# A third of the first out-projection moved into the mLSTM, and the S5 phasor table mirrored by another engine

## The chip, the cores and the metric

The kernel runs on one core of one Trainium2 chip. The metric is device time in microseconds for one execution. The engines are TensorE (PE in the profile; its weight loads are PEld), VectorE (DVE), ScalarE (ACT), GpSimd (POOL) and SyncE (SP, which here only issues DMAs); all run their own queue of instructions in order and wait for each other by semaphores.

## The reference

One inference step of a two-layer encoder for two request groups: a prompt of 2048 tokens behind 16 meta tokens, and 8 decode streams of 16 tokens. Layer 0 runs an S5 state-space mixer (512 columns wide) and an mLSTM (1024 columns wide) side by side; layer 1, retention and RG-LRU, is untouched by the change. What matters here:

```python
def even_layer(h, g, i, st, P, segments):
    u = rmsnorm(h, g)
    ua, za, xb, zb = jnp.split(u @ P['ev_w_in'][i], [W_A, 2 * W_A, 2 * W_A + W_B], axis=-1)
    ya, s_re, s_im = s5_mixer(ua, ...)
    yb, mc, mn, mm, mbuf = mlstm_mixer(xb, ...)
    gated = jnp.concatenate([ya * jax.nn.silu(za), yb * jax.nn.silu(zb)], axis=-1)   # 512 + 1024 columns
    h = h + gated @ P['ev_w_out'][i]                                                 # (1536, 1024)
```

The mLSTM is a recurrence over chunks of tokens with a 256x256 state per head and four heads. The out-projection's 1536 rows are 12 blocks (k) of 128: k 0 to 3 are the S5 third, k 4 to 11 belong to the mLSTM.

## The kernel before

The kernel is written as a sequence of phases inside one `tile.TileContext(schedule_with_timeline_sim=True)`: a scheduler with a simulated timeline sets the order of the instructions on each engine, the pools' buffers set what must wait for what. In the profile the phases lie at: `phase_in0` 0 to about 247 us (first in-projection), the S5 scan and the mLSTM's projections to about 885, `phase_mlstm` about 893 to 1203, `phase_out0` to about 1620, then layer 1.

**Number format.** Products that need more than one pass are split: `split` casts an operand to fp32r on ScalarE (`h`) and subtracts on VectorE or GpSimd (`l`), and `mm3` (L123 to L125) does three matmuls: h x h, h x l, l x h.

**The phasor table.** In `phase_in0`, at its second block, `s5_turns` builds for the S5 scan a table of rotations in four rounds of 8 groups. In each, VectorE fills the upper half of `s5tb` by repeated complex products (L557 to L562), ScalarE writes the mirrored lower half in two instructions (L744), and a DMA of 1032 KB in ScalarE's queue stores it to `d_rot` (L745). The pool of `s5tb` is closed after that, and its memory goes, among others, to `wfh`/`wfl`, the first split weights of the next phase, which therefore wait for the last store. ScalarE also issues the many `d_ua` stores (L305) at the end of the phase; SyncE issues the loads of the next phase (`wr`, `wv`, `ut`, `bif`), and GpSimd subtracts its split weights (L118).

**The mLSTM.** `phase_mlstm` goes over 17 tiles of 128 tokens, one in unit 0 and two in each of units 1 to 8. `ml_scores` of the next unit is written ahead of `ml_heads` of the current one. `ml_scores` does 48 matmuls of 256 columns (L123 to L125 on `m_xch`/`m_xcl`), transposes (L1214) and the score product (L1231); `ml_heads` does, for each of four heads, the output product into `pn` (L1361, L1363), two updates `pc` of the state `ct` (L1366, read by VectorE at L1370), the normalisation on VectorE and GpSimd (L1247 to L1255) and, at the end of a tile, eight transposes of `m_yn` into `pa` (L1269), which VectorE reads at L1272. The PSUM buffers are three `pn`, two `pc` and three `pa`. The split weights `wo0` to `wo3` of the out-projection are loaded in units 2 to 5 and those of k 4 to 7 in the last one. Behind the units come k 0 to 7 of the first out-projection tile (`e.first`, on `m_xc`) and the final state (L1426, eight pairs of products through `pc`).

**The out-projection.** `phase_out0` goes over the 17 tiles (and the 16 meta tokens) in the order that `out_tiles` gives. For a tile `out_operands` loads the 12 blocks (k 0 to 3 from `d_ya`, the rest from `d_gb`, L1466) and splits them, and `out_mm` does 2 halves x 12 k x 3 matmuls of 512 columns. `put` adds the residual on VectorE (L1502) and stores the tile to `d_h`. In the same loop the decode streams' mLSTM step (`ml_running`) advances by one piece for each of the first tiles: it loads the states `m_c` (L1307), updates and stores them, and GpSimd copies their columns to `ncol` (L1330). From the 13th tile on parts of the next in-projection take its place.

## Time and profile before

| what | value |
|---|---|
| time, median of 3 runs (lowest, highest) | 3130.14 us (3120.72, 3131.16) |
| the profiled execution | 3125.61 us |
| its span | 3123.9 us |
| TensorE busy | 2995.7 us, 96% of the span |
| VectorE, ScalarE, GpSimd busy | 1717.8 us (55%), 1062.8 us (34%), 970.9 us (31%) |
| DMA traffic | 404.82 MB, mean 130 GB/s |

The profiled execution is one run of its own; its time is 1.7 us more than the span that the trace covers. A busy share is an average over stages with different limits, so the stretches of the trace are read one by one below. The granted clock of TensorE has two levels, 2.4 GHz (1.00 in the profile) and 1.2 GHz; a mean between them says for how much of a stretch each held.

### The profile page before, as it was taken

The numbers are of one execution on the slowest core, as the hardware profiler recorded it, in microseconds if no ns is written. First come the engines' busy times: TensorE is split into PE (matmuls) and PEld (weight loads), VectorE is DVE, ScalarE is ACT, GpSimd is POOL, SyncE is SP. The second block draws the span as 40 slices with busy tenths as digits, with TensorE's granted clock in tenths as the row PEclk, the third lists the DMA queues.
The fourth block names the chain that finished last, engine by engine and source line by source line (L and its number), as shares of the span: only waits on it lengthen the run. The fifth ranks groups of instructions, "written<-read, shape, count | busy, mean of one in ns | idle before, by whom it ended". The sixth has DMA issues, their size and how long they took to land.

```text
span 3123.9 us, 45398 instructions
## 1 busy us (share of the span) xinstructions
PE 2995.7 (96%) x17435; PEld 2709.9 (87%) x17435; DVE 1717.8 (55%) x3482; ACT 1062.8 (34%) x1868; POOL 970.9 (31%) x1152
## 2 busy tenths in 40 slices
PE   8996999998999899999999999999999999999999
PEld 8996998997988887767799999999998898888887
DVE  4275885554547885233356666766610026665664
ACT  4223343335244433211235555555521112211221
POOL 6104664546436654111102111111100014433432
PEclk9998999998989999999999999999999999999999
DMA  6437555557634545665541111111122158544442
GB/s 214 120 100 210 158 168 151 164 165 159 209 91 149 171 153 171 212 196 169 152 147 59 48 49 52 51 52 52 43 84 75 52 157 249 140 127 131 135 124 75
DMA packets 447299, 404.82 MB, mean 130 GB/s; under 512 B 43593, under 2 KB 392977, under 8 KB 447082
## 3 DMA queue, kind: packets, MB, share of 16 engines
q1 hardware_dynamic: 335340, 272.36, 30.6%
q10 hardware_dynamic: 111742, 129.56, 12.4%
q8 instruction: 137, 2.24, 0.3%
q14 instruction: 80, 0.66, 0.1%
HBM read 266.35 MB, written 135.49 MB: 129 GB/s over the span
## 4 chain that ended last, share of the span: by engine, by line
PE 60%; DVE 8%; DMA 3%; issue 1%; ACT 1%; POOL 0%; SPq 0%; DVEq 0%; ACTq 0%; POOLq 0%
PE p_pm L124 8%; PE p_pm L125 8%; PE p_pm L123 8%; PE r_pm L125 4%; PE r_pm L124 4%; PE r_pm L123 4%; PE pa L123 3%; PE pa L124 3%; PE pa L125 3%; DVE p_d L1714 1%; PE pn L1363 1%; PE pc L1366 1%; DMA m_rw<-d_grow 1%; PE r_o L1916 1%; DVE m_qs L1206 1%
## 5 line engine op out<-in xcount | busy, mean ns | idle before, releaser
L123 PE MATMUL p_pm<-pu,p_wh 128*128 128x384 f32 (+1 forms) x1568 | 512.1, 327 | 0.2 <-ACT pu L105 0.2
L124 PE MATMUL p_pm<-pu,p_wh 128*128 128x384 f32 (+1 forms) x1568 | 511.8, 327 | 0.0
L125 PE MATMUL p_pm<-pu,p_wl 128*128 128x384 f32 (+1 forms) x1568 | 511.3, 326 | 0.0
L123 PE MATMUL pm<-ub,wh 128*128 128x384 f32 (+1 forms) x1136 | 378.6, 334 | 1.6 <-ACT vo L453 1.6
L124 PE MATMUL pm<-ub,wh 128*128 128x384 f32 (+1 forms) x1136 | 377.6, 332 | 1.6 <-DVE ub L109 1.6
L125 PE MATMUL pm<-ub,wl 128*128 128x384 f32 (+1 forms) x1136 | 375.2, 332 | 0.0
L123 PEld LDWEIGHTS p_pm<-pu,p_wh 128*128 128x128 f32 x1568 | 294.2, 188 | 1.8 <-issue 1.2
L124 PEld LDWEIGHTS p_pm<-pu,p_wh 128*128 128x128 f32 x1568 | 294.5, 188 | 1.0 <-issue 0.8
L125 PEld LDWEIGHTS p_pm<-pu,p_wl 128*128 128x128 f32 x1568 | 294.4, 188 | 0.0
L118 POOL TENSOR_TENSOR wl<-wr,wh 128x256 fp32r<-128x256 f32 x188 | 174.7, 959 | 222.4 <-ACT wh L105 222.4
L123 PEld LDWEIGHTS pm<-ub,wh 128*128 128x128 f32 x1136 | 216.3, 191 | 6.6 <-issue 4.0
L124 PEld LDWEIGHTS pm<-ub,wh 128*128 128x128 f32 x1136 | 216.3, 190 | 3.0 <-DVE ub L109 2.1
L124 PE MATMUL r_pm<-rol,r_gh 128*128 128x512 f32 x544 | 217.7, 401 | 1.1 <-POOL rol L109 0.6
L123 PE MATMUL r_pm<-roh,r_gh 128*128 128x512 f32 x544 | 217.9, 401 | 0.8 <-ACT p_o L1624 0.8
L125 PE MATMUL r_pm<-roh,r_gl 128*128 128x512 f32 x544 | 217.0, 400 | 0.7 <-DVE r_gl L109 0.7
L125 PEld LDWEIGHTS pm<-ub,wl 128*128 128x128 f32 x1136 | 215.9, 190 | 1.7 <-issue 1.6
L109 POOL TENSOR_TENSOR p_wl<-p_wr,p_wh 128x1024 fp32r<-128x1024 f32 x34 | 82.1, 2417 | 384.1 <-ACT p_wh L105 373.1
L109 POOL TENSOR_TENSOR p_xcl<-p_xc,p_xch 128x384 fp32r<-128x384 f32 (+1 forms) x48 | 46.8, 974 | 244.7 <-ACT p_xch L105 208.1
L125 PEld LDWEIGHTS r_pm<-roh,r_gl 128*128 128x128 f32 x544 | 102.9, 189 | 22.6 <-DVE r_gl L109 1.2
L124 PEld LDWEIGHTS r_pm<-rol,r_gh 128*128 128x128 f32 x544 | 102.9, 189 | 21.6 <-POOL rol L109 1.0
L123 PEld LDWEIGHTS r_pm<-roh,r_gh 128*128 128x128 f32 x544 | 102.7, 189 | 21.7 <-ACT p_o L1624 1.2
L1714 DVE RECIPROCAL p_d<-p_d 128x384 f32<-128x384 f32 (+1 forms) x48 | 116.7, 2430 | 0.6
(732 smaller groups left out, 6821.6 us busy)
## 6 DMA issues: line engine op xcount, KB each, us to landing
wr<-in_ev_w_in_dram SPq DMA_DIRECT2D x47, 512.0 KB
p_wr<-in_od_w_in_dram SPq DMA_DIRECT2D x40, 512.0 KB
d_in<-p_o ACTq DMA_DIRECT2D x80, 192.0 KB
m_rw<-d_grow SPq DMA_DIRECT2D x18, 512.0 KB
s5u<-d_ua SPq DMA_DIRECT2D x32, 274.0 KB
d_v<-vo ACTq DMA_DIRECT2D x68, 128.0 KB
m_va<-d_v SPq DMA_DIRECT2D x17, 512.0 KB
d_h<-o_x ACTq DMA_DIRECT2D x17, 512.0 KB
```

Of the source, the lines that this page charges most:

```text
L109: (nc.gpsimd if pool else nc.vector).tensor_tensor(l, x, h, op=OP.subtract)
L118: nc.gpsimd.tensor_tensor(out[:, c], a[:, c], b[:, c], op=op)
L123: nc.tensor.matmul(out, a[0], b[0], start=start, stop=False, **kw)
L124: nc.tensor.matmul(out, a[0], b[1], start=False, stop=False, **kw)
L125: nc.tensor.matmul(out, a[1], b[0], start=False, stop=stop, **kw)
L1206: v.tensor_tensor(qs[:, 4 * j:4 * j + 4, :n].rearrange("p (h m) n -> p h m n", m=2), qt[j][:, :, cs].rearrange("p (h m) n -> p h m n", m=2 ...
L1363: nc.tensor.matmul(pn[:n], c.qs[:, 2 * h + k, :n], ct[h][:, k, :], start=False, stop=k == 1)
L1366: nc.tensor.matmul(pc, c.kw[:n, h, 128 * k:128 * (k + 1)], c.va[:n, h, :], start=True, stop=True)
L1714: v.reciprocal(d[:, :n], d[:, :n])
L1916: nc.tensor.matmul(po, qk[:, h, :], S[:, h, :], start=False, stop=True)
```

## The change

The S5 third of the out-projection is computed tile by tile inside the mLSTM. `first_part`, called once for each of the 17 tiles after its unit's heads, loads the tile of `d_ya` (256 KB), splits it on ScalarE and VectorE, does 2 halves x 4 k x 3 matmuls of 512 columns into a new PSUM buffer `pf`, copies each half with ScalarE, and stores it (ScalarE's queue) to a new DRAM tensor `d_hp`. The room in PSUM comes from `pc`, which has one buffer instead of two. The weights `wo0` to `wo3` are loaded ahead of the units. In the out-projection only k 4 to 11 remain; each tile loads its rows of `d_hp` (512 KB, L1514 of the new kernel) and GpSimd adds them to the residual (L1515). In `s5_turns` the mirror is done by GpSimd, and the store is issued by SyncE.

```diff
@@ s5_turns
             for i in range(2):
-                nc.scalar.mul(tb[:, i, :, 0:MID][:, :, ::-1], tb[:, i, :, MID + 1:], 1.0 - 2 * i)
-            nc.scalar.dma_start(e.rot[:, :, gs, :], tb)
+                nc.gpsimd.tensor_scalar(tb[:, i, :, 0:MID], tb[:, i, :, MID + 1:][:, :, ::-1], 1.0 - 2 * i, None,
+                                        op0=OP.mult)
+            nc.sync.dma_start(e.rot[:, :, gs, :], tb)
@@ -1385,10 +1386,31 @@
         wo.append((h, l))
 
     with P(e, "m_sb", 2) as sb, PS(e, "m_ps") as ps:
-        pn, pa = psum(ps, pn=3, pc=2), psum(e.pa, pa=3)
+        pn, pa = psum(ps, pn=3, pc=1, pf=1), psum(e.pa, pa=3)
         pt = lambda nm, *shape: (pa if nm == "pa" else pn)(nm, *shape)
         units = [[1]] + [[s, s + 1] for s in range(2, 18, 2)]
         nxt = ml_scores(e, sb, lp, ow0, pt, units[0])
+        for k in range(4):
+            r = sb.tile([128, D], F32, name="m_zb", bufs=2)
+            nc.sync.dma_start(r, out_w(e)[:, k, :])
+            weights(k, r, *(ow0.tile([128, D], F32R, name=f"wo{x}{k}") for x in "hl"))
+
+        def first_part(c0, n, kind, row):
+
+            g = sb.tile([128, 4, 128], F32, name="m_fg")
+            h, l = (sb.tile([128, 4, 128], F32R, name="m_f" + x) for x in "hl")
+            nc.sync.dma_start(g, e.ya[:, :, c0:c0 + n])
+            split(nc, h, l, g)
+            for q in range(2):
+                qs = slice(512 * q, 512 * q + 512)
+                pf = pn("pf", 512)
+                for k in range(4):
+                    mm3(nc, pf, (h[:, k], l[:, k]), (wo[k][0][:, qs], wo[k][1][:, qs]), k == 0, k == 3)
+                o = sb.tile([128, 512], F32, name="m_fo")
+                nc.scalar.copy(o, pf)
+                nc.scalar.dma_start(e.hp[c0:c0 + n, qs], o)
+
+        rest = out_tiles(e)
         for i in range(len(units)):
             cur = nxt
             if i + 1 < len(units):
@@ -1404,16 +1426,12 @@
                         weights(k + j, r[:, j, :], *(ow0.tile([128, D], F32R, name=nm, bufs=b) for _ in range(2)))
             for c in cur:
                 ml_heads(e, c)
-            if 2 <= i < 6:
-
-                r = sb.tile([128, D], F32, name="m_zb", bufs=2)
-                nc.sync.dma_start(r, out_w(e)[:, i - 2, :])
-                weights(i - 2, r, *(ow0.tile([128, D], F32R, name=f"wo{x}{i - 2}") for x in "hl"))
+                first_part(*rest.pop(0))
         t = out_tiles(e)[0]
         e.first = out_operands(e, lambda j, nm: lp.tile([128, 12, 128], F32 if nm == "g" else F32R, name="m_xc",
                                                         bufs=3), 1, *t)
         e.pms = [pa("pa", 512) for _ in range(2)]
-        for k in range(8):
+        for k in range(4, 8):
             for q in range(2):
                 out_mm(e, e.pms[q], t[1], e.first, k, q)
 
@@ -1457,21 +1475,21 @@
 
 def out_operands(e, room, parts, c0, n, kind, row):
 
-    m = 12 // parts
+    m = 8 // parts
     r = []
     for j in range(parts):
         g, h, l = (room(j, nm) for nm in "ghl")
         for k in range(0, m, 4):
             f = m * j + k
-            e.nc.sync.dma_start(g[:, k:k + 4, :n], e.gb[:, f - 4:f, c0:c0 + n] if f else e.ya[:, :, c0:c0 + n])
-        split(e.nc, h[:, :, :n], l[:, :, :n], g[:, :, :n])
+            e.nc.sync.dma_start(g[:, k:k + 4, :n], e.gb[:, f:f + 4, c0:c0 + n])
+        split(e.nc, h[:, :m, :n], l[:, :m, :n], g[:, :m, :n])
         r += [(h[:, k, :n], l[:, k, :n]) for k in range(m)]
     return r
 
 
 def out_mm(e, pm, n, g, k, q):
     qs = slice(512 * q, 512 * q + 512)
-    mm3(e.nc, pm[:n], g[k], (e.wo[k][0][:, qs], e.wo[k][1][:, qs]), k == 0, k == 11)
+    mm3(e.nc, pm[:n], g[k - 4], (e.wo[k][0][:, qs], e.wo[k][1][:, qs]), k == 4, k == 11)
 
 
 DSTEPS = 1
@@ -1491,7 +1509,10 @@
 
         def residual(c0, n, kind, row):
             h1 = sb.tile([128, D], F32, name="o_x")
+            hp = sb.tile([128, D], F32, name="o_hp")
             nc.sync.dma_start(h1[:n], src_rows(e, kind, row, n))
+            nc.sync.dma_start(hp[:n], e.hp[c0:c0 + n, :])
+            nc.gpsimd.tensor_tensor(h1[:n], h1[:n], hp[:n], op=OP.add)
             return h1
 
         def put(c0, n, h1, pms):
@@ -1530,11 +1551,11 @@
 
         acc = lambda: e.pa.tile([128, 512], F32, name="pa", bufs=3)
 
-        ops = [e.first, out_operands(e, room, 3, *tiles[1])]
+        ops = [e.first, out_operands(e, room, 2, *tiles[1])]
         ops_ = opn(e, "o_ps", side="right", psum=True)
         pms = [e.pms, [acc(), ops_.tile([128, 512], F32, name="o_p")]]
         e.wo += split_weights(e, wp, out_w(e), range(8, 12), D, "wo", sb, "o_x")
-        for i, k in [(1, k) for k in range(8)] + [(i, k) for k in range(8, 12) for i in range(2)]:
+        for i, k in [(1, k) for k in range(4, 8)] + [(i, k) for k in range(8, 12) for i in range(2)]:
             for q in range(2):
                 out_mm(e, pms[i][q], tiles[i][1], ops[i], k, q)
         cls(e, "m_ld")
@@ -1565,10 +1586,10 @@
             if i == P1N:
                 e.w3 = [p1_weights(e, 128 * m) for m in range(3)]
                 p1_norm(e, 4, nwb, psn, 2)
-            g, h1 = out_operands(e, room, 3, *t), residual(*t)
+            g, h1 = out_operands(e, room, 2, *t), residual(*t)
             pm = [acc() for _ in range(2)]
             for q in range(2):
-                for k in range(12):
+                for k in range(4, 12):
                     out_mm(e, pm[q], t[1], g, k, q)
             put(t[0], t[1], h1, pm)
     cls(e, "ps_n", "m_pa", "o_w0")
...
+    e.hp = dram.tile([T, D], F32, name="d_hp")
```

How the order of the instructions moves is shown at three places. A row is a line of the kernel (its own, so that L1366 of before is L1367 after), an operation, output and inputs, the shape, and a count where rows in a row are alike.

SyncE's queue at the start of the phase behind `phase_in0`, before (`ut` are tiles of the input, `wr` and `wv` weights, `s5u` and `s5rt` the S5 scan's inputs):

```order
L380 DMA wr_3057<-in_ev_w_in_dram 128x8x128
L468 DMA ut_4954<-d_u 128x8x128
L442 DMA wv_3501<-in_ml_wv_dram 128x2x256
L468 DMA ut_5951<-d_u 128x8x128
L753 DMA s5u<-d_ua 128x548 x2
L771 DMA s5rt<-d_rot 128x2x516
```

and after:

```order
L380 DMA wr_3058<-in_ev_w_in_dram 128x8x128
L468 DMA ut_4955<-d_u 128x8x128
L442 DMA wv_3502<-in_ml_wv_dram 128x2x256
L468 DMA ut_5952<-d_u 128x8x128
L746 DMA d_rot<-s5tb 256x1x1032
L754 DMA s5u<-d_ua 128x548 x2
L772 DMA s5rt<-d_rot 128x2x516
```

The fourth store of the table, which stood in ScalarE's queue, now stands behind the last of the seven `ut` loads; the first three stand together ahead of `bif`.

GpSimd at the same place, before:

```order
L408 MEMSET xb_2604 128x3
L443 COPY wv_2931<-gw 128x2x8
L118 TENSOR_TENSOR wl_2676<-wr_2673,wh_2675 128x256 x4
L118 TENSOR_TENSOR wl_2743<-wr_2740,wh_2742 128x256 x4
L118 TENSOR_TENSOR wvl_2935<-wv_2931,wvh_2934 128x264 x2
L443 COPY wv_3501<-gw 128x2x8
```

and after:

```order
L744 TENSOR_SCALAR s5tb<-s5tb 128x8x64 x6
L408 MEMSET xb_2605 128x3
L443 COPY wv_2932<-gw 128x2x8
L118 TENSOR_TENSOR wl_2677<-wr_2674,wh_2676 128x256 x4
L118 TENSOR_TENSOR wl_2744<-wr_2741,wh_2743 128x256 x4
L118 TENSOR_TENSOR wvl_2936<-wv_2932,wvh_2935 128x264 x2
L744 TENSOR_SCALAR s5tb<-s5tb 128x8x64 x2
L443 COPY wv_3502<-gw 128x2x8
```

Three rounds of the mirror stand ahead of the subtractions of the split weights, the fourth behind all ten of them.

TensorE within one of the last units of the mLSTM, before (`ident` with `m_xc` or `m_yn` are transposes, `m_qt` with `m_xc` the scores):

```order
L1214 MATMUL pa<-ident,m_xc 128x128 x4
L1231 MATMUL pa<-m_qt,m_xc 128x128 x8
L1214 MATMUL pa<-ident,m_xc 128x128 x4
L1366 MATMUL pc<-m_va,m_kw 128x258 x2
L1361 MATMUL pn<-m_va,m_p 128x258
L1363 MATMUL pn<-ct_8299,m_qs 128x258 x2
L1214 MATMUL pa<-ident,m_xc 128x128 x4
L1361 MATMUL pn<-m_va,m_p 128x258
L1363 MATMUL pn<-ct_8300,m_qs 128x258 x2
L1366 MATMUL pc<-m_va,m_kw 128x258
L1231 MATMUL pa<-m_qt,m_xc 128x128 x8
L1366 MATMUL pc<-m_va,m_kw 128x258
```

and after, in unit 5 or later:

```order
L1232 MATMUL pa<-m_qt,m_xc 128x128 x8
L1367 MATMUL pc<-m_va,m_kw 128x258
L1362 MATMUL pn<-m_va,m_p 128x258
L1364 MATMUL pn<-ct_8300,m_qs 128x258
L1367 MATMUL pc<-m_va,m_kw 128x258
L1364 MATMUL pn<-ct_8300,m_qs 128x258
L1362 MATMUL pn<-m_va,m_p 128x258
L1367 MATMUL pc<-m_va,m_kw 128x258
L1364 MATMUL pn<-ct_8301,m_qs 128x258
L1367 MATMUL pc<-m_va,m_kw 128x258
L1364 MATMUL pn<-ct_8301,m_qs 128x258
L1215 MATMUL pa<-ident,m_xc 128x128 x8
```

The two `pc` of a head, which stood together, now stand with a `pn` product between them where there is one; right behind these rows comes a run of four `pc`.

TensorE in unit 4 after the change, at the end of the last of the 34 groups of moved matmuls:

```order
L123 MATMUL pf<-woh_9075,m_fh 128x512
L124 MATMUL pf<-wol_9076,m_fh 128x512
L125 MATMUL pf<-woh_9075,m_fl 128x512
L1367 MATMUL pc<-m_va,m_kw 128x258
L1364 MATMUL pn<-ct_8300,m_qs 128x258
L1367 MATMUL pc<-m_va,m_kw 128x258 x2
L1270 MATMUL pa<-ident,m_yn 128x128 x8
L1367 MATMUL pc<-m_va,m_kw 128x258
L1362 MATMUL pn<-m_va,m_p 128x258
L1364 MATMUL pn<-ct_8301,m_qs 128x258 x2
```

Behind it no `pf` is left, though the loop calls `first_part` in every unit: the scheduler has pulled the matmuls of the later tiles forward, where they stand singly or in rows of several groups between the `pc` and `pn` products of units 0 to 4.

## Rows read from the trace of the kernel before

**Rows 1.** The page, part 1: busy us (share of the span) x instructions.

```profile
PE 2995.7 (96%) x17435; PEld 2709.9 (87%) x17435; DVE 1717.8 (55%) x3482; ACT 1062.8 (34%) x1868; POOL 970.9 (31%) x1152
```

**Rows 2.** Windows: stretch, its length, busy us by engine, granted clock, DMA share, GB/s.

```profile
core 0: us, PE busy (x) PEld busy (x) DVE busy (x) ACT busy (x) POOL busy (x), PEclk, DMA share, GB/s
247.00:271.00 24.00, 0.46 (x3) 0.46 (x3) 12.62 (x43) 9.88 (x14) 7.44 (x8) 0.59 1.02 311
...
893.00:940.00 47.00, 45.73 (x268) 36.71 (x269) 21.55 (x70) 23.46 (x52) 19.00 (x24) 0.82 0.25 73
940.00:1000.00 60.00, 54.57 (x325) 47.38 (x324) 48.79 (x160) 23.43 (x53) 32.00 (x46) 1.00 0.42 130
1000.00:1060.00 60.00, 55.02 (x328) 49.78 (x329) 49.60 (x136) 25.78 (x51) 39.76 (x43) 0.91 0.58 175
1060.00:1160.00 100.00, 88.75 (x515) 78.89 (x514) 84.33 (x242) 40.53 (x83) 58.95 (x69) 0.93 0.49 150
1160.00:1203.00 43.00, 36.08 (x177) 29.12 (x176) 38.43 (x121) 14.17 (x29) 25.11 (x32) 0.88 0.57 167
...
1260.00:1300.00 40.00, 40.00 (x221) 31.66 (x220) 9.09 (x15) 11.95 (x30) 4.63 (x9) 1.00 0.72 232
1300.00:1500.00 200.00, 200.00 (x1042) 140.76 (x1041) 73.19 (x163) 33.54 (x70) 29.12 (x93) 1.00 0.56 172
```

**Rows 3.** Waits of PE, 930 to 1215: us in total, times, longest.

```profile
PE pa L123 <- DVE m_g L1272: 17.3, 5, 3.5
PE pc L1366 <- DVE ct L1370: 4.1, 3, 1.7
```

**Rows 4.** Timeline of PE: start, length, instruction [idle before, releaser].

```profile
1110.96 0.38 PE L123 MATMUL pa<-m_xch,amh 128*128 128x256 f32 x1 [3.45 <-DVE m_g L1272]
...
1330.01 0.39 PE L124 MATMUL pa<-wol,o_gh 128*128 128x512 f32 x1
1330.24 0.39 PE L125 MATMUL pa<-woh,o_gl 128*128 128x512 f32 x1
```

**Rows 5.** Groups of ACT by form, 940 to 1203: busy us, mean ns, idle before.

```profile
L1181 ACT COPY m_qt<-pa 128x512 f32<-128x512 f32 x24 | 14.0, 585 | 45.4 <-PE pa L125 45.4
```

**Rows 6.** Timelines of PE, DVE and POOL within a unit.

```profile
1094.48 1.04 PE L1366 MATMUL pc<-m_va,m_kw 128*128 128x258 f32 x4
...
1089.38 1.29 DVE L1206 TENSOR_TENSOR m_qs<-m_qt,m_rw 128x512 f32<-128x512 f32 x2 [0.58 <-DMA m_rw<-d_grow]
1095.12 0.92 DVE L1370 SCALAR_TENSOR_TENSOR ct<-ct,m_rw,pc 128x258 f32<-128x258 f32 x2 [0.69 <-PE pc L1366]
1106.04 3.71 DVE L1206 TENSOR_TENSOR m_qs<-m_qt,m_rw 128x512 f32<-128x512 f32 x2
...
1105.81 2.35 POOL L1274 TENSOR_TENSOR m_zb<-m_g,m_zb 128x1024 f32<-128x1024 f32 x1 [3.01 <-DVE m_g L1272]
```

**Rows 7.** Groups of PE by form, 1260 to 1500.

```profile
L123 PE MATMUL pa<-woh,o_gh 128*128 128x512 f32 x172 | 69.6, 404 | 0.0
```

**Rows 8.** Waits of SP's DMA queue, 1203 to 1620.

```profile
SPq L1307 <- DMA out_dram<-m_c: 56.0, 20, 9.9
SPq L1466 <- DVE o_gl L109: 53.9, 22, 6.3
```

**Rows 9.** Timeline of ACT at the seam to the out-projection.

```profile
1238.78 1.05 ACT L105 CAST woh<-o_x 128x1024 fp32r<-128x1024 f32 x1 [3.50 <-DMA o_x<-in_ev_w_out_dram]
```

**Rows 10.** Timelines of ACT, POOL, SP and PE around the last store of the table.

```profile
245.82 0.49 ACT L233 ACTIVATE zst<-pm 128x384 f32<-128x384 f32 x1 [6.13 <-DMA d_ua<-uas]
...
264.05 0.52 ACTq L745 DMA_DIRECT2D d_rot<-s5tb  x1
...
269.45 1.04 ACT L105 CAST wfh<-xt 128x1024 fp32r<-128x1024 f32 x1 [1.12 <-DMA d_rot<-s5tb]
...
263.56 8.48 POOL L118 TENSOR_TENSOR wl<-wr,wh 128x256 fp32r<-128x256 f32 x8 [16.90 <-ACT wh L105]
...
275.91 0.52 SPq L468 DMA_DIRECT2D ut<-d_u  x1
...
270.55 0.59 PE L123 MATMUL pm<-ub,wfh 128*128 128x272 f32 x1 [23.54 <-ACT wfh L105]
```

## The prediction

> **What bounds the kernel now.** I read the busy shares of the page first, then busy time, clock and DMA by stretch, then what TensorE waits for in the mLSTM, then its timeline with VectorE's and ScalarE's beside it.
>
> TensorE is busy for 96% of the span [rows 1], so the time is TensorE's work plus the few places where it idles or runs at the lower clock. The stretches show two such places [rows 2]. At 247 to 271 us it works 0.46 us of 24. In the mLSTM, 893 to 1203 us, it is busy 45.73, 54.57, 55.02, 88.75 and 36.08 us of 47, 60, 60, 100 and 43: 29.9 us idle. Its mean granted clock there is 0.82, 1.00, 0.91, 0.93 and 0.88; busy time times the missing share is 8.2 + 0 + 5.0 + 6.2 + 4.3 = 23.7 us. So at most 54 us are to be had inside the mLSTM. In the out-projection, 1260 to 1500, it is busy without a gap at full clock.
>
> What it waits for in the mLSTM is VectorE: 17.3 us in five stalls of up to 3.5 us before the next unit's scores, and only 4.1 us for the state buffer `pc` [rows 3]. In one such stall TensorE comes back at 1110.96 after 3.45 us [rows 4].
>
> The profiled execution took 3125.61 us, 1.7 us more than its span; the median of the runs is 4.5 us above it. The sum is made against 3125.61.
>
> **The moved matmuls.** Per tile 2 halves x 4 k x 3 = 24 matmuls of 512 columns go from the out-projection to the mLSTM, 408 in all. One costs a step of 0.23 us (1330.01 to 1330.24 [rows 4]), so 93.8 us leave one phase and enter the other. What counts is how much of it falls into idle time, and what the new buffers and queues cost.
>
> *What the fill absorbs.* The order decides where it can: all 34 groups of 12 (`pf`) stand ahead of the last pair of `pc` in unit 4, some of them several in a row, and units 5 to 8 have none. Unit 4 ends in the trace of before near 1060. Up to there idle time is 1.3 + 5.4 + 5.0 = 11.7 us and the clock's loss 8.2 + 0 + 5.0 = 13.2 us [rows 2], together 25. The weights of k 0 to 3 must be loaded, cast and subtracted before the first group, so part of the first 47 us stays as it was. I take **-22** (ends -26 and -10). The other 29 us, after 1060, get no cover.
>
> *Its single PSUM buffer.* A group of 12 lasts 2.76 us; then `pf` must be copied by ScalarE before the next group may start. A 128x512 copy from PSUM takes 585 ns [rows 5]; between groups mostly one `pc` and one `pn` product stand, about 0.87 us, so a copy on time is just covered, and each time ScalarE is behind a 1.05 us cast it is not. I take 0.2 us for each of 34: **+7** (ends 0, and 25 when nothing of the copy and its handover is covered).
>
> *`pc` with one buffer instead of two.* Now a `pc` product waits until VectorE has read the one before. In the trace two products start at 1094.48 (four records, 0.436 us a product) and the reader starts at 1095.12 after a wait for the product; two readers take 0.92 us [rows 6]. With 0.44 for the product, 0.47 for the read and about 0.18 for each handover, an estimate from these rows, one buffer turns round in about 1.27 us against 0.44, so a `pc` that follows another at once costs 0.83. In a bare unit the new order has a run of four `pc`, one of two, and two places with only one product between: 4 x 0.83 + 2 x 0.4 = 4.1 us. Some of it lies in waits for VectorE that exist anyway; one `pc` also stands behind the pair of `m_qs` products, which took 3.71 us at 1106.04 against 1.29 at 1089.38 [rows 6]. I take 2.8 us for each of 4.3 bare units: **+12** (ends 0 and 22). In the filled units the groups stand between the `pc` and hide it.
>
> The Trainium skill (GPSIMD Engine Reference, section 8, Key points) says that GpSimd shares its SBUF interfaces with VectorE and contends with VectorE instructions that have two SBUF inputs. The trace agrees: the slow pair lies beside a 2.35 us GpSimd product at 1105.81 [rows 6]. By the rule the 17 new subtractions of the split would be stretched too; GpSimd is busy 59% of 940 to 1203 and one overlap cost 2.4 us, so 17 x 0.59 x 2.4 = 24 us more VectorE work, which would add nothing while TensorE is the later one in a filled unit, and up to those 24 us if it isn't.
>
> *The tail.* After unit 8 the new order has five `pc` in a row and then the eight pairs of products of the final state through one buffer, with 24 instead of 48 matmuls of the first tile as cover: 4 x 0.83 + 3 = **+6** (ends 0 and 12).
>
> **The out-projection.** 93.8 us go, since TensorE has no gap there. What replaces them: per tile 256 KB of `d_ya` less but 512 KB of `d_hp` more, and a 128x1024 addition on GpSimd, whose like takes 2.35 us [rows 6]; 17 of them are 40 us on an engine busy 29 us of 200, hidden unless they hold up the `ncol` copies that free the decode states. Casts and subtractions fall from 12 to 8 parts a tile, which helps. In 1300 to 1500 the DMAs move 172 GB/s [rows 2]. A tile has 16 matmuls of L123 on `woh` (k 0 to 3 and 8 to 11); 172 of them in 240 us [rows 7] are 22.3 us a tile, so 3.8 MB. Without 24 matmuls it would last about 16.8 us and need 4.1 MB, 244 GB/s. Before, 232 was held over 1260 to 1300 [rows 2]. The load queue has its waits already: 56.0 us for states to be written, 53.9 us for VectorE's split [rows 8]. At the seam, the last weights (k 11) are cast at 1238.78 after a wait for their load [rows 9], and TensorE comes there 5 to 11 us earlier now. I take 5 for the seam and 3 for the queues: **+8** (ends 0 and 45).
>
> **The phasor table.** Today TensorE stops for 23.54 us until 270.55, because the cast `wfh` at 269.45 writes over `s5tb` and waits for the fourth `d_rot` store, issued by ScalarE at 264.05 behind the mirror; the third mirror had come late, behind ScalarE's `d_ua` stores, for which it last waited 6.13 us before 245.82 [rows 10]. GpSimd was idle then, and if its mirrors came on time, that wait and the two copies after it, some 8 us, could go. But the third store, now SyncE's, uses a slot for which a `d_ua` store issued near 245 must have finished, so it doesn't leave earlier. And in GpSimd's order the fourth mirror now stands behind ten subtractions, of which the first eight take 8.48 us [rows 10]; today they begin at 263.56, when ScalarE has cast the weights, and in the new order they can begin near 257, as ScalarE no longer waits for VectorE there, and end near 269. The mirror itself isn't in the trace: at least ScalarE's 0.6 us apiece, at most the subtraction's 1.06. So it is done near 271 against 264. The store then stands behind the last of seven `ut` loads on SyncE, issued at 275.91 today [rows 10], some 5 us sooner if the subtractions are. It leaves at 271 to 276 instead of 264.05. I take **+7** (ends -8, if the subtractions hold up nothing, and +12).
>
> **The sum.** -93.8 + 93.8 - 22 + 7 + 12 + 6 + 8 + 7 = +18. 3125.6 + 18 = **3144 us** forecast. Against the median that is within 0.5% (3114.5 to 3145.8, about what a measurement can tell from no change), near its upper edge.
>
> **The rivals.** *A gain.* VectorE paces the bare units (84.33 us busy of 100 at 1060 to 1160 [rows 2]), so what `pc` waits is taken from stalls that exist; `pf` and the out-projection are hidden. Then -26 and, for the phasor table, 0 remain: 3100; with the 8 us of the phasor table 3092. For it speaks that only 4.1 us were lost at `pc` [rows 3]; against it, that this was with two buffers.
>
> *Slower: the decode tiles become DMA-bound.* If the load queue, with its waits on stores and splits, doesn't pass 200 GB/s, each of about 12 tiles takes 20.5 us instead of 16.8: +44 instead of the 3 for the queues, 3185. It decides below 244 GB/s. For it: 172 GB/s now, with 110 us of waits in the queue. Against: 232 in one stretch, 311 at 247 to 271 [rows 2].
>
> *Slower by the clock.* In the stretches with the stalls the mean granted clock is 0.91, 0.93 and 0.88 of 2.4 GHz [rows 2], so for a part of them it is at the lower level of 1.2. If the short waits at the single `pc` kept bringing it down, the 4.3 bare units (150 us, 130 busy) at 0.82 instead of 0.92 would lose 13 us, with stalls of 4.1 instead of 2.8 another 6: 3163. The Trainium skill (TensorE: Matmul & The Clock Gate, Part 1, "A second HAM failure mode: psum-queue depth-cycling") describes a kernel whose clock went up and down because TensorE idled shortly while cycling through PSUM banks. Against it, no stall at `pc` in the trace lasted over 1.7 us [rows 3].
>
> **Chances.** Forecast (3120 to 3165) 0.42, gain 0.32, DMA-bound 0.17, clock 0.09. Faster by over 0.5%: 0.9 of the gain and a little of the forecast, 0.31. Within: half of the forecast and the rest of the gain, 0.24. Slower: 0.45. The range runs from the gain with the phasor table's 8 us to the DMA case: 3092 to 3185.
>
> **What would show it.** In the profile after: `pf` products all before unit 5; the stretch of units 1 to 4 busy at full clock; waits of `pc` for `ct` in units 5 to 8, some 12 us in all instead of 4.1; the first product with `wfh` near 277; in the out-projection, tiles of 17 to 18 us at 230 GB/s or more. It is wrong if the `pc` waits merely replace those for `m_g`, if the fourth mirror comes before 264, or if TensorE idles in the decode tiles.

## The result

The changed kernel takes 3235.18 us (median of 4 runs, 3233.51 to 3239.68) against 3128.39 for the kernel before in the same comparison: a ratio of 1.0346, 95% interval 1.0327 to 1.0365. It is 107 us slower. The forecast was 3144 us with a range up to 3185; the sign of the sum was right, its size was not.

The profiled execution of after has a span of 3231.8 us. Page, part 1 (as rows 1), and what TensorE waits for over the whole span (waits: us in total, times, longest):

```profile
PE 3022.1 (94%) x17435; PEld 2712.6 (84%) x17435; DVE 1721.2 (53%) x3483; ACT 1074.4 (33%) x1895; POOL 1018.2 (32%) x1177
```

```profile
PE pm L123 <- ACT wfh L105: 36.1, 1, 36.1
PE pc L1367 <- DVE ct L1371: 30.0, 25, 3.1
PE pa L123 <- ACT o_gh L105: 18.7, 1, 18.7
...
PE pa L123 <- DVE m_g L1273: 12.4, 4, 3.5
...
PE pf L123 <- ACT m_fo L1410: 0.5, 2, 0.2
```

TensorE does the same 17435 instructions. Against [rows 3, 10] the wait for `wfh` grew from 23.5 to 36.1 us, that at `pc` from 4.1 to 30.0, and a new one of 18.7 us stands in the out-projection. The buffer `pf`, to which the prediction gave 7 us, cost 0.5.

Where the 108 us of span lie is read from four starts on TensorE (in both traces):

| start of | before | after | later by |
|---|---|---|---|
| the first product with `wfh` | 270.55 | 282.48 | 11.9 |
| the first score product of unit 1 | 902.4 | 925.6 | 23.2 |
| the last `pc` of the mLSTM | 1202.6 | 1364.8 | 162.2 |
| the first product of the next in-projection | 1563.8 | 1671.8 | 108.0 |
| end of span | 3123.9 | 3231.8 | 107.9 |

So 23 us are lost by the start of the mLSTM's loop, 139.0 - 93.8 = 45 in it beyond the moved matmuls, and the out-projection, which gave up 93.8 us of matmuls, became only 54.2 shorter: 40 lost. The windows of after (columns as rows 2) show the three kinds of stretch:

```profile
1000.00:1050.00 50.00, 47.98 (x262) 41.21 (x263) 28.96 (x75) 17.68 (x36) 20.75 (x21) 1.00 0.50 148
...
1200.00:1250.00 50.00, 41.28 (x227) 34.81 (x227) 31.00 (x95) 16.13 (x33) 24.75 (x30) 0.91 0.40 119
...
1450.00:1500.00 50.00, 50.00 (x282) 33.21 (x280) 22.02 (x41) 9.46 (x20) 19.79 (x29) 1.00 0.74 238
1500.00:1550.00 50.00, 50.00 (x262) 33.30 (x262) 24.44 (x49) 9.28 (x21) 15.21 (x32) 1.00 0.82 261
1550.00:1600.00 50.00, 50.00 (x253) 34.95 (x252) 20.64 (x44) 10.35 (x23) 14.97 (x31) 1.00 0.63 211
...
1600.00:1650.00 50.00, 31.00 (x161) 22.70 (x159) 13.53 (x36) 4.68 (x12) 13.46 (x27) 0.82 0.52 165
```

A filled unit (1000 to 1050) keeps TensorE at 96% and full clock; a bare one (1200 to 1250) has it at 83%, worse than the 89% of [rows 2]; the out-projection's tiles (1450 to 1600) run without a gap at 211 to 261 GB/s, and then TensorE stands for 19 us.

Measured from the first score product of a unit to that of the next (the columns name the two units), TensorE took:

| us | 1 to 2 | 2 to 3 | 3 to 4 | 4 to 5 | 5 to 6 | 6 to 7 | 7 to 8 |
|---|---|---|---|---|---|---|---|
| before | 24.9 | 37.7 | 36.5 | 36.0 | 37.0 | 36.5 | 36.0 |
| after | 32.6 | 76.6 | 62.0 | 57.8 | 44.9 | 45.3 | 44.1 |

The first four stretches took 94.0 us more, and all but 2 us of the 93.8 us of moved matmuls stand in them: against before, the fill absorbed nothing net. The three bare ones took 8.3 us more each, and from there to the last `pc` 75.9 instead of 55.7.

### The profile page after: what moved, and what is told of

Read it like the earlier page. It is cut to its first block, busy times and chain, and to the rows that moved or that the text cites. A ratio compares the mean times of both kernels' runs of the same rounds, so it can differ in the third digit from the quotient of the medians.

```text
span 3231.8 us, 45561 instructions
## 1 busy us (share of the span) xinstructions
PE 3022.1 (94%) x17435; PEld 2712.6 (84%) x17435; DVE 1721.2 (53%) x3483; ACT 1074.4 (33%) x1895; POOL 1018.2 (32%) x1177
## 4 chain that ended last, share of the span: by engine, by line
PE 73%; DVE 12%; DMA 9%; issue 2%; ACT 2%; ACTq 1%; POOL 1%; SPq 0%; DVEq 0%; POOLq 0%
PE p_pm L124 8%; PE p_pm L125 8%; PE p_pm L123 8%; PE pm L123 4%; PE pm L124 4%; PE pm L125 4%; PE r_pm L125 4%; PE r_pm L124 4%; PE r_pm L123 4%; PE pa L123 2%; PE pa L124 2%; PE pa L125 2%; DMA m_rw<-d_grow 2%; PE pc L1367 1%; DVE p_d L1735 1%
## 5 line engine op out<-in xcount | busy, mean ns | idle before, releaser
L1371 DVE SCALAR_TENSOR_TENSOR ct<-ct,m_rw,pc 128x258 f32<-128x258 f32 x128 | 61.5, 480 | 114.8 <-PE pc L1367 113.8
L125 PEld LDWEIGHTS r_pm<-roh,r_gl 128*128 128x128 f32 x544 | 102.8, 189 | 23.2 <-DVE r_gl L109 1.8
L1367 PE MATMUL pc<-m_va,m_kw 128*128 128x258 f32 (+1 forms) x272 | 91.2, 418 | 32.3 <-DVE ct L1371 30.0
```

Source lines behind the costliest of these rows:

```text
L125: nc.tensor.matmul(out, a[1], b[0], start=False, stop=stop, **kw)
L1367: nc.tensor.matmul(pc, c.kw[:n, h, 128 * k:128 * (k + 1)], c.va[:n, h, :], start=True, stop=True)
L1371: nc.vector.scalar_tensor_tensor(ct[h][:, k, :], ct[h][:, k, :], c.rw[:, 1, h, 127:128], pc, op0=OP.mult, op1=OP.add)
```

## Theories, and the experiments

Theory: the one `pc` buffer is the main loss in the mLSTM, in filled and bare units alike; the phasor part costs the store's delay; the out-projection's loss has its cause at its end, where TensorE waits for `o_gh`. Rivals: the moved matmuls' own traffic and splits, a slower clock, or a VectorE that paces the units whatever TensorE is given.

### The phasor part undone, and alone

e1_ph_old: the changed kernel with the two statements of before in `s5_turns`. e2_ph_only: the kernel before with this edit alone.

```diff
-                nc.scalar.mul(tb[:, i, :, 0:MID][:, :, ::-1], tb[:, i, :, MID + 1:], 1.0 - 2 * i)
-            nc.scalar.dma_start(e.rot[:, :, gs, :], tb)
+                nc.gpsimd.tensor_scalar(tb[:, i, :, 0:MID], tb[:, i, :, MID + 1:][:, :, ::-1], 1.0 - 2 * i, None,
+                                        op0=OP.mult)
+            nc.sync.dma_start(e.rot[:, :, gs, :], tb)
```

Expected of e1: 

> The changed kernel with the mirror and its store put back on ScalarE. After, the first product with wfh came at 282.48 instead of 270.55 us, 11.9 us late. Theory A (the phasor part costs what it moves that product by, and nothing else): about 12 us less than after, 3223 us, and the wait before that product is back at 23.5 us. Rival B (the queues that it moved also cost the next phase, where after lost another 16 us up to the first mLSTM state product): 20 to 28 us less, 3207 to 3215. Rival C (the stall is hidden later by work that waits anyway): within 5 us of after.

Expected of e2: 

> The kernel before with the phasor part alone. Theory A: 12 us more than before, about 3140, with the wait before the first product with wfh near 36 us. Rival B: 20 to 28 us more, 3148 to 3156. Rival D (in the kernel before the order of GpSimd and SyncE comes out otherwise and the fourth mirror comes on time): 8 to 11 us less, 3118.

e1 took 3228.38 us, ratio 1.0317 (1.0302 to 1.0332); e2 took 3144.43, ratio 1.0048 (1.0033 to 1.0063), 15 us more than before (3129.07). In e2 TensorE waits 35.9 us for `wfh`, in e1 24.1. So the part by itself costs 12 us in its stall and some more behind it, nearest to theory A. In e1 the first product of the next in-projection came 11.6 us sooner than in after, but the whole only 7, between theory A and rival C; the stretch behind that product differs by up to 6 us between the profiles of these builds.

The chain in after (timelines of POOL, SP, ACT and PE) runs through the steps that the prediction had drawn:

```profile
258.95 5.98 POOL L118 TENSOR_TENSOR wl<-wr,wh 128x256 fp32r<-128x256 f32 x8 [11.85 <-ACT wh L105]
...
266.68 4.01 POOL L744 TENSOR_SCALAR s5tb<-s5tb 128x512 f32<-128x512 f32 x2
...
273.97 1.35 SPq L746 DMA_DIRECT2D d_rot<-s5tb  x1
...
281.38 1.04 ACT L105 CAST wfh<-xt 128x1024 fp32r<-128x1024 f32 x1 [15.48 <-DMA d_rot<-s5tb]
...
282.48 0.59 PE L123 MATMUL pm<-ub,wfh 128*128 128x272 f32 x1 [36.10 <-ACT wfh L105]
```

The subtractions begin earlier than in [rows 10], at 258.95, but the fourth mirror stands behind them and ends at 270.69 (forecast: near 271); the store waits behind the `ut` loads until 273.97 (forecast: 271 to 276; before, 264.05), and the cast starts 7.4 us after that, where it was 5.4.

That 270.69 met the forecast is partly luck. The subtractions were done at 266.7, sooner than the 269 forecast, and the two mirrors took 4.0 us instead of about 2. And the queue was not alone in holding the mirror: VectorE's own fourth round, which fills the half that is mirrored, ended 5.1 us later than in before. It began at the same time (254.13 and 254.14), but beside GpSimd's subtractions, which now fall into it, its products took two to three times as long, until the subtractions were done. Its last products, before and after:

```profile
262.25 0.42 DVE L561 TENSOR_TENSOR s5r<-s5tb,s5pp 128x256 f32<-128x256 f32 x1
262.71 0.42 DVE L562 TENSOR_TENSOR s5tb<-s5r,s5r 128x256 f32<-128x256 f32 x1
```

```profile
266.91 0.83 DVE L561 TENSOR_TENSOR s5r<-s5tb,s5pp 128x256 f32<-128x256 f32 x1
267.77 0.42 DVE L562 TENSOR_TENSOR s5tb<-s5r,s5r 128x256 f32<-128x256 f32 x1
```

The second of the two mirrors, which starts at 268.3, needs this last product, which ends at 268.2. So with VectorE as slow as this, it could have started no sooner with an empty queue ahead of it. No run has the mirror ahead of the subtractions.

### One pc buffer alone

e3_pc1: the kernel before with one number changed.

```diff
-        pn, pa = psum(ps, pn=3, pc=2), psum(e.pa, pa=3)
+        pn, pa = psum(ps, pn=3, pc=1), psum(e.pa, pa=3)
```

Expected of e3: 

> The kernel before with one buffer of pc in the mLSTM instead of two and nothing else. Prediction's price (2.8 us for each of 8 units, 6 for the tail): 28 us more, 3156. Theory from the profile after (units without moved matmuls lasted 44 to 45 us instead of 36.5, and the tail some 12 us more): 8 x 8.2 + 12 = 78 us more, 3206. Rival (the longer units came from the moved matmuls' DMAs and splits, not from pc): under 10 us more.

e3 took 3206.16 us, ratio 1.0239 (1.0220 to 1.0257), 77 us more. The theory from the profile after is borne out, the prediction's 28 us is not. The scheduler orders the mLSTM anew for one buffer: on TensorE the order differs from that of before between 901 and 1299 us and nowhere else, so the run shows the cost of the buffer together with the order that comes with it. The stretches of the table above are 24.2, 48.8, 44.1, 44.5, 44.9, 44.7 and 44.4 us in e3; the last five, without a single moved matmul, are like the bare ones of after. From the first score product of unit 1 to the last `pc` it is 75.7 us longer than before. Its waits of TensorE:

```profile
PE pc L1366 <- DVE ct L1370: 34.6, 30, 3.1
...
PE pa L123 <- DVE m_g L1272: 18.5, 6, 3.4
```

The wait at `pc` is added to the one for `m_g`, which stays (17.3 us in [rows 3]); it doesn't replace it. The mean clock over the last five stretches is 0.94, against 0.95 before, so the clock has next to no part in it (windows of before, then of e3):

```profile
965.00:1146.90 181.90, 161.88 (x962) 143.86 (x960) 154.81 (x437) 75.69 (x158) 114.92 (x132) 0.95 0.52 159
```

```profile
983.00:1206.00 223.00, 177.70 (x961) 144.68 (x961) 149.04 (x437) 73.94 (x154) 112.06 (x131) 0.94 0.43 128
```

The run also tells what the fill did. The single buffer alone makes the first four stretches 26.6 us longer (161.6 against 135.0), and those of after, which hold some 92 us of moved matmuls, are 67 us longer than these. So with the buffer already paid for, about 24 us of the fill were absorbed, an estimate from two profiles whose orders differ.

In the tail of after the turn-round can be read off the timeline of TensorE, where five `pc` stand in a row:

```profile
1358.50 0.70 PE L1367 MATMUL pc<-m_va,m_kw 128*128 128x258 f32 x2 [0.36 <-DVE ct L1371]
1359.92 0.70 PE L1367 MATMUL pc<-m_va,m_kw 128*128 128x258 f32 x2 [0.72 <-DVE ct L1371]
1361.20 0.70 PE L1367 MATMUL pc<-m_va,m_kw 128*128 128x258 f32 x2 [0.58 <-DVE ct L1371]
1362.48 1.14 PE L1367 MATMUL pc<-m_va,m_kw 128*128 128x258 f32 x2 [0.58 <-DVE ct L1371]
```

1.28 us from start to start in two steps, 1.42 in the first: the estimate of 1.27 was right. Of these 1.28 only 0.58 are told as a wait, since the row of the product itself lasts 0.70; so the sums of waits understate the cost. What was wrong is how often and how long VectorE's read is late. I priced only neighbours in the order; but VectorE's queue holds other work between two reads (normalisation, the `m_qs` pair), and a product that waits for it holds up everything behind it. In e3 the long waits are seven of 2.8 to 3.1 us, 20.6 of the 34.6, and all seven look like this one (timelines of SP, DVE and PE):

```profile
1045.28 0.57 SPq L1197 DMA_DIRECT2D m_rw<-d_grow  x1
...
1050.18 1.29 DVE L1206 TENSOR_TENSOR m_qs<-m_qt,m_rw 128x512 f32<-128x512 f32 x2 [2.00 <-DMA m_rw<-d_grow]
1051.39 0.48 DVE L1370 SCALAR_TENSOR_TENSOR ct<-ct,m_rw,pc 128x258 f32<-128x258 f32 x1
...
1051.92 0.70 PE L1366 MATMUL pc<-m_va,m_kw 128*128 128x258 f32 x2 [2.98 <-DVE ct L1370]
```

The read of `pc` stands behind the two `m_qs` products, and these wait for the load of `m_rw`, which lands 4.9 us after its issue. With two buffers all waits at `pc` were 4.1 us [rows 3], and `m_qs` waited for its load 0.58 us at 1089.38 [rows 6]; why the load comes later for VectorE in e3 was not taken apart. The other waits are mostly single turn-rounds of 0.58. It happens in a filled unit too (timelines of PE, DVE and ACT in after):

```profile
1063.72 0.70 PE L1367 MATMUL pc<-m_va,m_kw 128*128 128x258 f32 x2 [2.60 <-DVE ct L1371]
1064.07 0.58 PE L123 MATMUL pf<-woh,m_fh 128*128 128x512 f32 x1
...
1061.98 1.29 DVE L1207 TENSOR_TENSOR m_qs<-m_qt,m_rw 128x512 f32<-128x512 f32 x2 [3.70 <-DMA m_rw<-d_grow]
1063.19 0.48 DVE L1371 SCALAR_TENSOR_TENSOR ct<-ct,m_rw,pc 128x258 f32<-128x258 f32 x1
...
1061.98 1.28 ACT L1222 ACTIVATE m_w<-m_rw,acol 128x128 f32<-128x128 f32 x4 [2.10 <-DMA m_rw<-d_grow]
1063.16 0.56 ACT L1410 COPY m_fo<-pf 128x512 f32<-128x512 f32 x1
```

TensorE waits 2.60 us for `pc` with a group of twelve `pf` matmuls right behind it, and the group covers nothing of the wait. It couldn't have started sooner in any case: ScalarE waits for the same load, and its copy frees `pf` at 1063.72, the moment at which `pc` comes free. Two other groups of after stand so, at 1001.7 and 1126.3.

By the splits nothing was lost that shows: the 17 subtractions of `m_fl` took 0.67 to 0.69 us each, so none was stretched, where the prediction had allowed up to 24 us.

The Trainium skill (Trainium Kernel Development and Optimization, Best Practices, point 5) says that "consistent bubbles can mean SBUF/PSUM ran out". The trace agrees: in e3 30 waits of up to 3.1 us stand at the one PSUM buffer that was left.

### The moved matmuls with pc's second buffer kept

e5_pfpn: after, phasor part as before, `pf` taken from `pn`'s buffers. e7_pa: the same with `pa`'s, and with the edit of e6 below.

```diff
-        pn, pa = psum(ps, pn=3, pc=1, pf=1), psum(e.pa, pa=3)
+        pn, pa = psum(ps, pn=3, pc=2), psum(e.pa, pa=3)
...
-                pf = pn("pf", 512)
+                pf = pn("pn", 512)
```

Expected of e5: 

> The changed kernel with the phasor part of before and with the moved matmuls in the buffers of pn (three) instead of one of their own, so that pc keeps its two. In the order they now stand as four groups in every unit instead of thirty in units 1 to 4. Theory A (the single pc buffer and the crowding are what the mLSTM lost): units back to 36.5 us plus 11 us of matmuls minus the 3.5 us stall and its slow clock, 42 to 44 us; with out0 as after (39 us short of what it gave up) about 3217 - 34 (bare units) - 12 (tail) - 25 (fill in every unit) = 3146, at most 3165. Rival (VectorE paces the units and the fill only lengthens them): units of 47 us or more, 3190 or more.

e5 took 3168.84 us, ratio 1.0126 (1.0109 to 1.0142): 60 us less than e1, just above the bound that theory A had set, since units last 45 to 49 us rather than 42 to 44, so that some meet the rival's 47. The shared buffers also spread the groups, four a unit, so this run changes two things at once; e3 had told the buffer apart. One unit in the middle still costs about 10 us more than before for 11.0 us of matmuls.

Expected of e7: 

> The kernel of e6 with the moved matmuls in the buffers of pa (which the scores and transposes share) instead of pn. In the order they stand as four groups a unit, as in e6. If what counts is only that pc keeps two buffers and the groups are spread: within 6 us of e6. If the groups delay whoever shares their buffers: other than e6 by over 10 us; for pa the scores of the next unit, which are the ones that wait for VectorE's m_g, would wait for ScalarE's copy of the group too, so slower.

e7 took 3152.06 us, ratio 1.0086 (1.0053 to 1.0119), 16 us less than e6. Faster, where I had expected the same or slower: from unit 3 on its units last 43.4 to 43.9 us, so 7 us more than before for 11 us of matmuls. Which buffers the fill borrows matters, but why `pa` is better than `pn` was not taken apart; the 11.4 us of waits at `pc` in e5 are 7.7 here.

### The end of the out-projection

e6_last: e5 with the loads of the next in-projection written behind the last tile's operands. e9_end: the same edit on e1.

```diff
-P1B, P1N = 12, 15
+P1B, P1N = 12, 16
...
+            g, h1 = out_operands(e, room, 2, *t), residual(*t)
             if i == P1N:
                 e.w3 = [p1_weights(e, 128 * m) for m in range(3)]
                 p1_norm(e, 4, nwb, psn, 2)
-            g, h1 = out_operands(e, room, 2, *t), residual(*t)
```

Expected of e6: 

> The kernel of e5_pfpn with one thing moved: the loads and norms of the next in-projection (p_wr) are written behind the operand loads of the last out-projection tile instead of ahead of the 16th tile, so that in SyncE's order the last tile's two o_g loads stand ahead of the p_wr loads, which wait for the decode's last store. In e5 TensorE stood 18.7 us for that tile's o_gh and came back at the lower clock. Theory (head of the queue): the o_g loads leave some 12 us sooner; 12 to 25 us less than e5, 3144 to 3157. Rival (the stall only moves on to the p_wr weights, which get their room when the decode ends): within 6 us of e5, 3163 or more.

Expected of e9: 

> The changed kernel with the phasor part of before (as e1) and the same move of the p_wr loads as in e6, the moved matmuls as in the change. Theory (the end of the out-projection lost its cover because the tiles became shorter, whatever the mLSTM does): 12 to 25 us less than e1, 3203 to 3216. Rival: within 6 us of e1.

e6 took 3168.27 us, ratio 1.0130 (1.0108 to 1.0153), e9 3230.12, 1.0325 (1.0301 to 1.0349): no gain in either, though in e6 the wait for `o_gh` is 14.6 us instead of 18.7. My theory of the queue falls. The timelines of e6 (ACT, SP, PE) show why:

```profile
1568.63 0.54 ACTq L1275 DMA_DIRECT2D d_gb<-m_rw  x1
...
1572.17 0.92 SPq L1483 DMA_DIRECT2D o_g<-d_gb  x2
...
1575.81 0.80 PE L123 MATMUL pa<-m_xch,o_gh 128*128 128x512 f32 x1 [14.62 <-ACT o_gh L105]
```

The `o_g` loads are first in the queue now, and still leave 3.5 us after the store of `d_gb`: the last tile is the decode streams' own, and its operands are the result of `ml_running`. TensorE waits for the decode itself. Before, the order holds 222 matmuls of 512 columns behind the decode's last state product, 51 us of cover; after, and in every kernel with all 17 tiles moved, 48, which are the last tile's own. In the trace of before that product is at 1508.4 and TensorE goes on without a gap; in after it is at 1631.1:

```profile
1640.30 0.54 ACTq L1276 DMA_DIRECT2D d_gb<-m_rw  x1
...
1645.03 1.98 SPq L1484 DMA_DIRECT2D o_g<-d_gb  x2
...
1651.48 0.79 PE L123 MATMUL pa<-m_xch,o_gh 128*128 128x512 f32 x1 [18.70 <-ACT o_gh L105]
```

### Fewer tiles, later weights

e8_late: e6 with the weights of k 0 to 3 loaded in units 0 and 1, the tiles moved in units 2 to 8. e11_late17: the same on e7, with other numbers. e12_seven and e13_ten: as e11 with seven and ten tiles moved; the others keep all 12 blocks in the out-projection, and `d_hp` is added in halves. Parts of the edit of e12:

```diff
             for c in cur:
                 ml_heads(e, c)
-                first_part(*rest.pop(0))
+            for k in range(2 * i, 2 * i + 2) if i < 2 else ():
+                ...
+            for _ in range((0, 0, 1, 1, 1, 1, 1, 1, 1)[i]):
+                first_part(*rest.pop(0))
...
-            g, h1 = out_operands(e, room, 2, *t), residual(*t)
+            mv = i < 7
+            g, h1 = out_operands(e, room, 2 if mv else 3, *t), residual(*t, moved=mv)
```

Expected of e8: 

> The kernel of e6 with the weights of k 0 to 3 loaded and split in units 0 and 1 (two each) instead of ahead of all units, and the moved matmuls in units 2 to 8 (two tiles a unit, three in the last three). In e5 TensorE waited 7.3 us for the gates (m_w) behind VectorE, whose queue holds the weights' subtractions there, and the stretch up to 940 us ran at clock 0.70. Theory (loading the weights ahead of the units costs the start): 8 to 15 us less than e6. Rival (the same VectorE work only comes later, and the crowded last units give back what the start gains): within 6 us of e6, or more.

e8 took 3165.96 us, ratio 1.0121 (1.0095 to 1.0146): as e6. The start did gain (the first two stretches are back at 25.0 and 37.7 us, the first score product comes at 906.7 instead of 914.8), and the crowded end, with three tiles a unit, gave it back: the rival's case.

Expected of e11: 

> The kernel of e7_pa (all 17 tiles moved, in the buffers of pa, pc with two, phasor part of before) with the weights loaded in units 0 and 1 and the moved tiles in units 2 to 8 (3, 3, 3, 2, 2, 2, 2). In TensorE's order 48 matmuls of 512 columns stand behind the decode's last state product, as in every kernel with all tiles moved; in the kernel before there are 222. Theory (the out-projection's loss is the decode's end, which the shorter tiles no longer cover): the stall before the last tile stays at 13 to 19 us, and only the start gains, 8 to 15 us less than e7, 3137 to 3144. Rival (the crowded units give that back): 3150 or more.

e11 took 3149.64 us, ratio 1.0069 (1.0051 to 1.0086), 2 us less than e7: within what two comparisons can tell apart, less than the theory said and close to its rival. The stall before the last tile is 13.8 us, as said.

Expected of e12: 

> As e11, but only seven tiles are moved, one in each of units 2 to 8; the other ten keep all 12 blocks in the out-projection. 220 matmuls stand behind the decode's last state product. Theory (a unit has room for about one tile, some 4 to 5 us, and with the cover kept the out-projection gives back what left it): the stall before the last tile is gone, units of 37 to 39 us instead of 36.5, mLSTM 7 x 5.5 - 25 to -30 = 9 to 14 us longer, out-projection 7 x 5.5 = 38 us shorter: 20 to 30 us less than before, 3100 to 3110. Rival (fill and cover don't add up; each switch between fp32 and fp32r products and the added loads cost what the fill gains): within 8 us of before.

e12 took 3114.51 us, ratio 0.9952 (0.9933 to 0.9970): faster than both kernels, by 14 us (0.5%) where I had expected 20 to 30. No wait for `o_gh` is left. Windows and waits of e12:

```profile
1004.00:1154.00 150.00, 146.59 (x869) 127.88 (x868) 118.67 (x351) 62.56 (x133) 92.45 (x105) 1.00 0.53 162
```

```profile
PE pc L1366 <- DVE ct L1370: 5.6, 8, 1.7
...
PE pa L123 <- DVE m_g L1272: 5.2, 6, 3.6
```

TensorE is busy 98% at full clock there, units last 37.2 us with 5.5 us of moved matmuls in each, 0.8 more than before (the first unit with fill 41.2, 5.2 more), and the 17.3 us of waits for `m_g` are down to 5.2. So the mLSTM's half of the theory held: from the first score product of unit 1 to the last `pc` it is 7.6 us longer for 38.6 us of matmuls, where 9 to 14 were expected. The out-projection's half did not: up to the next in-projection it is only 29.1 us shorter than before, not 38.6. TensorE idles for 6.3 us there, against 1.6 before; the rest was not taken apart.

Expected of e13: 

> As e12 with ten tiles moved (2, 2, 2, 1, 1, 1, 1 in units 2 to 8); 150 matmuls behind the decode's last state product. Theory: the cover still holds (150 x 0.23 = 35 us against a stall of 19), the three added tiles bring little each since their units are full: within 5 us of e12. Rival (the cover is already too short): 10 us or more over e12, with a wait for o_gh.

e13 took 3123.45 us, ratio 0.9988 (0.9976 to 1.0000), 9 us more than e12 and without a wait for `o_gh`, between theory and rival. The cover holds; the added tiles cost: the three units with two tiles last 46.8, 46.6 and 42.6 us, and those with one 41.0 and 37.0. A unit has room for about one tile.

## Why the prediction was wrong

**Right in mechanism.** TensorE bounds the out-projection but for its end, the fill is pulled into units 0 to 4, bare units pay for `pc`, the phasor table's store comes later and not sooner.

**`pc` with one buffer: the step that failed most.** The sum had 2.8 us for each of 4.3 bare units and nothing for the filled ones. e3 shows some 8.1 us a unit from unit 3 on. The turn-round was right (1.28 against 1.27 us), but I took off a third for waits "that exist anyway", and they are added: 34.6 us at `pc` beside 18.5 for `m_g`. I had seen that one `pc` stands behind the `m_qs` pair, but not that the pair waits for a load: that alone is 20.6 of the 34.6 us. And I let `pf` hide it in the filled units, where a waiting `pc` stands ahead of the `pf`; by e3 the single buffer costs 26.6 us in the first four stretches. In after the three bare stretches lost 24.8 us (12 forecast) and the tail 20 (6 forecast; from the start of unit 8's scores to the last `pc`, of which a unit's 8 leave about 12): together the mLSTM's 45 us. From unit 5's scores on the waits at `pc`, forecast at some 12 us, are 21.2. What speaks most for the gain rival, that only 4.1 us were lost at `pc` [rows 3], was a number with two buffers, and said nothing of one.

**The fill: -22 forecast, 0 against before, about 24 against e3.** The idle time of [rows 2] did close (96% busy, full clock), but the single `pc` took as much back. The term itself was about right; what the sum lacked is the price of `pc` in the same units. With two buffers and one tile a unit 4.7 of 5.5 us are absorbed (e12, units of 37.2); with two tiles about 4 of 11 (e7).

**`pf`'s own buffer: +7 forecast, 0.5 us of waits measured.** ScalarE was mostly on time; where it came over 3 us late (three groups, as at 1063.16), the wait at `pc` lies over it.

**The start.** Not in the sum: 11 us between the phasor stall and the first score product. e1 without the phasor part still has 7 of them, and in after TensorE waits 7.1 us for the gates (`m_w`) where it was 2.4 in before. e8 gets 8 us back with later weights. Some of the 11 may be scatter: e3, whose edit lies behind it, needs 6 us more than before from the phasor stall to that product.

**The out-projection: +8 forecast, +40 measured.** I looked for DMA and queue limits; TensorE runs without a gap from 1450 to 1600 at 238, 261 and 211 GB/s, about the 244 below which the DMA rival decides, so that rival falls. The step that failed here is "93.8 us go, since TensorE has no gap there": with tiles a third shorter the decode's result was the last thing to arrive. 18.7 us are that wait; the rest lies in the return at a mean clock of 0.82 to 0.90 (1600 to 1700), and at the seam, where the final state's products wait 5.4 us at the single buffer and the clock is at 0.83 (1350 to 1400). From the last `pc` to the next in-projection the windows of before, then of after, are:

```profile
1202.60:1563.80 361.20, 359.57 (x1810) 268.57 (x1810) 122.58 (x250) 75.89 (x158) 58.27 (x136) 1.00 0.59 184
```

```profile
1364.80:1671.80 307.00, 272.74 (x1372) 194.08 (x1370) 114.34 (x225) 65.28 (x141) 97.83 (x154) 0.93 0.71 231
```

TensorE idles for 34.3 us instead of 1.6, so some 33 of the 40 are idle time, and about 7 are left for the lower clock and the rest. How much the seam and the return give was not measured apart.

**The clock rival** falls as a cause in the mLSTM: e3 is 77 us slower with a mean clock of 0.94 in its units, against 0.95.

**The phasor table: +7 forecast, 12 us in the stall, 15 in the time (e2), 7 (e1).** The mirror took about 1.6 us a piece, 2.0 in the fourth round, not the 0.6 to 1.06 that the bounds had; VectorE's fourth round ended 5.1 us later, which the prediction took as unchanged; and the store's landing let the cast start 2 us later behind its issue. That the subtractions ended sooner than forecast made up for part of it.

## What to carry to other kernels

Before a PSUM buffer is taken away, look at all that stands between two uses in the reader's queue, and at what that waits for (here a load), not only at the neighbours in the writer's order: the wait was added to those that exist, and fill behind the waiting instruction didn't cover it. A phase without idle time on its bounding engine gives its work back only until the next chain through it is as long, so look at what arrives last there and keep its cover. Fill pays for the first few microseconds of a gap: seven tiles beat ten, seventeen and none.

## What the runs showed of the hardware

A GpSimd mirror of 128x512 (a product with 1 or -1, its input reversed) took about 1.6 us where ScalarE took 0.64:

```profile
243.78 3.13 POOL L744 TENSOR_SCALAR s5tb<-s5tb 128x512 f32<-128x512 f32 x2 [21.57 <-DVE s5tb L559]
```

The Trainium skill (GPSIMD Engine Reference, section 4.1, Engine selection) calls one-input elementwise work on GpSimd roughly line-rate; this mirror, with its reversed input, was slower than that reads, and in the fourth round it took 2.0 us.

VectorE's products of 128x256 took 0.83 to 0.94 us beside GpSimd's subtractions in the fourth round of after, and 0.42 in that of before.

A TensorE group of 512-column fp32r matmuls behind an fp32 product shows 0.42 us for its first step and 0.23 for the others. That is no cost of the switch. In after:

```profile
1056.43 0.60 PE L1364 MATMUL pn<-ct,m_qs 128*128 128x258 f32 x2
1056.68 0.58 PE L123 MATMUL pf<-woh,m_fh 128*128 128x512 f32 x1
1057.10 0.40 PE L124 MATMUL pf<-wol,m_fh 128*128 128x512 f32 x1
```

From the start of the fp32 product to the second matmul of the group it is 0.67 us, as much as 0.44 for a product [rows 6] and 0.23 for a matmul: the first matmul's record only starts earlier.
